# Roots of the norms on GpSimd, late transposes, quartered modulation products and token-by-token ends in a two-layer backbone

## The chip, the cores and the metric

One core of a Trainium2 chip runs the whole program. The metric is device time in microseconds (us), the median of three runs. TensorE (PE, with its weight loads PEld), VectorE (DVE), ScalarE (ACT), GpSimd (POOL) and SyncE (SP, which here only issues DMAs) each work through their own list of instructions in order; semaphores tie the lists together.

## What is computed

Two layers over 640 tokens of width 1024 (128 context tokens, 512 latent tokens). The first layer mixes tokens by attention and by a gated delta rule side by side, the second by a state-space mixer; each is followed by an MLP. Before every mixer and every MLP the tokens are normalised and modulated, and every result is gated into the residual. Cut to what the change touches:

```python
mod = silu(cond) @ w_mod[layer] + b_mod[layer]           # cond: one row for context, one for latent
sh1, sc1, g1, sh2, sc2, g2 = split(mod, 6)
h = rms_norm(x, norm_mix_g[layer]) * (1 + sc1) + sh1     # mean square, root, scale, shift
x = x + g1 * mixer(h)
h = rms_norm(x, norm_mlp_g[layer]) * (1 + sc2) + sh2
x = x + g2 * (square(relu(h @ w_mlp_in)) @ w_mlp_out)
```

After the second layer there is a last norm. The outputs are the tokens, the keys and values of the context, and the final states of both recurrences.

## The kernel before

**Products.** Every 32-bit operand is split into a rounded part and its remainder (`hh`/`hl` for activations, `whi`/`wlo` for weights), and a product is three matmuls. The rounding is a copy on ACT, the remainder a subtraction on DVE (a few on POOL). `stage` makes products that come out with features on partitions (tile `gps`, line 304): blocks of weights are the stationary side, and half of the tokens, 320 or 322 columns, move. The first half covers token tiles 0, 1 and half of 2. Twenty-four matmuls make one block of 128 features for one half.

**by_rows.** The projections back to the residual (`oute` and `outo` behind the mixers, `m2` in the MLP) come out with tokens on partitions (tile `rps`, line 330). The 1024 output columns are made in two halves `hm` of 512. Weights arrive as 1 MB blocks of four rows of 128, split into pairs. For each row and each of the five token tiles there are three matmuls. With `done` given and in the second half, the last eight rows are held, and then each token tile is finished by itself; in all other halves the five tiles grow side by side and finish together. Five of six PSUM banks are filled at a time.

**Norm and modulation.** As a token tile of the second half is finished, `gated` adds it to `x`, `square` sums its squares on ACT, and `done` goes on: after tile 1 (for 0 and 1), after tile 2, and after tile 4 (for 3 and 4) `root` makes the reciprocal roots by three Newton steps (`rsqrt`, lines 238 to 243, all on DVE, nine small operations behind two integer ones), `scaled` multiplies by root and scale (`hrow`, line 402) and adds the shift (line 403), and `turned` transposes eight blocks on PE (tile `hps`, line 409), four at a time, into `hh` (ACT, line 412) and `hl` (DVE, line 413). When tile 4 is done, all the transposes that are left are written into the program before the next stage. This happens at three places: between layer 0's mixer and its MLP (about 604 to 634 us), between the layers (1098 to 1130 us, where `hps` has one PSUM bank), and between layer 1's mixer and its MLP (1736 to 1760 us).

**Modulation vectors.** `mod_first` makes layer 0's first two with `condst`, 32 columns wide, as stationary side; it runs four 128-column quarters of the weights into four groups of 32 PSUM partitions (line 515). The other ones come from `mod_steps`, a generator that is advanced between other work and walks over chunks of 512 columns: two raw blocks of 1 MB each through two landing buffers. For chunks 4 to 9 of layer 0, in the stretch of the delta heads' input products, PE multiplies directly, eight matmuls of 512 columns into 32 partitions a chunk (line 462). For the other fourteen chunks, beside layer 0's MLP, ACT and DVE sum the products with the weights into two accumulators `macc` (four buffers, lines 486 and 489), and PE sums over partitions by two matmuls of 512 columns. `mod_out` adds bias and gain after each chunk and writes 4 KB to DRAM, from which `bands` broadcasts later.

**Layer 1's output projection.** `odd` first loads and splits weights, then makes `yh`/`yl` out of the mixer's result `yt`, and takes the mixer norm's mean squares by fifteen small matmuls (`stc`, line 1413) and its roots `yr` ahead of `by_rows`; `yr` is used in `gated`.

**What sets the order.** The program is written in the order of the code and then put in order for each engine by the framework's scheduler, which goes by its own estimate of times. So a change of one stage can also move instructions of another one.

Of the kernel before, what the change touches and what calls it, by code (L numbers as in the profile page):

```python
# [111 lines left out]
def _rows(i):  # L112

    out, index, pos = [], {}, 0

    def put(key, v):
        nonlocal pos
        index[key] = pos
        out.append(np.asarray(v).reshape(-1))
        pos += out[-1].size  # L120

    for layer in range(2):
        for c in range(12):
            put(("bias", layer, c), np.stack([i["b_mod"][layer, c * 512:c * 512 + 512]] * 2))
        for c in (2, 3, 8, 9):
            gain = i["norm_mix_g" if c < 4 else "norm_mlp_g"][layer]
            put(("gain", layer, c), np.stack([gain[c % 2 * 512:c % 2 * 512 + 512]] * 2))
    put("gfin", i["final_norm_g"])
    return np.concatenate(out), index
# [36 lines left out]
def _consts():  # L166
# [11 lines left out]
    put("ident", np.eye(P))  # L178
    put("stat", np.full((P, 1), 1.0 / 32.0))
# [28 lines left out]
class Prog:  # L208
    def __init__(self, nc, tc, ctx, io, widx, ridx, pidx, cidx, csmall, taps=None):
        self.nc, self.tc, self.ctx, self.io = nc, tc, ctx, io  # L210
        self.turn, self.share = 0, False
        self.behind = None
        self.mlast = None
        self.widx, self.ridx, self.pidx, self.cidx, self.csmall = widx, ridx, pidx, cidx, csmall
        self.taps = taps or {}
# [17 lines left out]
    def rsqrt(self, pool, out, ms, shape, post=1.0):  # L233
# [73 lines left out]
    def stage(self, keys, xs, half, evac, side=None):  # L307

        for i in range(0, len(keys), 2):
# [9 lines left out]
    def by_rows(self, keys, parts, evac, done=None, side=None, pre=()):  # L319
# [12 lines left out]
        for hm in range(2):  # L332
            banks, held = [], []
            for i, key in enumerate(keys(hm)):
# [39 lines left out]
    def norm_rows(self, pool):  # L374
# [8 lines left out]
        def root(a, b):  # L383
            v.scalar_tensor_tensor(out=ms[:, a:b], in0=ss[:, a:b, 0], scalar=EPS, in1=ss[:, a:b, 1], op0=ALU.add, op1=ALU.add)
            self.rsqrt(pool, r[:, a:b], ms[:, a:b], [P, b - a])
# [4 lines left out]
    def modulated(self, pool, scale, shift, h, off, halves):  # L390
# [6 lines left out]
        def scaled(t, r):  # L397
            q = min(t, 1)
            for j in range(2):
                y = halves(t, j)  # L400
                c = slice(j * 512, j * 512 + 512)
                v.scalar_tensor_tensor(out=y, in0=self.x[:, t, c], scalar=r[:, t:t + 1], in1=scale[:, q, c], op0=ALU.mult, op1=ALU.mult)
                v.tensor_tensor(out=y, in0=y, in1=shift[:, q, c], op=ALU.add)
                todo.append((t, 4 * j, y))

        def turned(t, a, y):
            ps = self.pn.tile([P, 512], F32, name="hps", tag="n")
# [7 lines left out]
        def done(t):  # L415
# [15 lines left out]
    def mod_bias(self, layer, c, pool):  # L431

        out = []
        for key in ("bias", "gain")[:2 if (layer, c) in self.gains else 1]:
            x = pool.tile([2, 512], F32, name=f"m{key}", tag=f"m{key}", bufs=2 if key == "bias" else 1)
            o = self.ridx[key, layer, c]
            self.nc.sync.dma_start(out=x, in_=self.io["rows"][o:o + 1024].rearrange("(p x) -> p x", p=2))
            out.append(x)
        return out

    def mod_out(self, layer, c, ps, row, gain=None):

        nc = self.nc
        nc.vector.tensor_tensor(out=row, in0=ps[0:2], in1=row, op=ALU.add)
        if gain is not None:
            nc.vector.scalar_tensor_tensor(out=row, in0=row, scalar=1.0, in1=gain, op0=ALU.add, op1=ALU.mult)
        nc.scalar.dma_start(out=self.modr[layer][c // 2, :, c % 2 * 512:c % 2 * 512 + 512], in_=row)

    def mod_steps(self, todo, landing, small, pool=None, after=None):
# [4 lines left out]
        if pool:  # L454
            sel = pool.tile([P, 2, 32], F32, name="msel")
            nc.vector.memset(sel, 0.0)
            for j in range(2):
                nc.vector.memset(sel[:, j, j:j + 1], 1.0)
        raws, n = [], 2 * len(todo)

        def product(lhs, x, start, stop):
            nc.tensor.matmul(ps, lhs, x, start=start, stop=stop)  # L462

        for i in range(n + 1):
            if i < n:
                layer, c = todo[i // 2]
                raw = landing.tile([P, 2048], F32, name="wraw", tag="wraw")
                o = self.widx["mod", layer, c, i % 2]
                nc.sync.dma_start(out=raw, in_=self.io["wall"][o:o + P * 2048].rearrange("(p x) -> p x", p=P))
                raws.append(raw.rearrange("p (k c) -> p k c", c=512))  # L470
                if i % 2 == 0:
                    nextrows = self.mod_bias(layer, c, small)
            if i:
                layer, c = todo[(i - 1) // 2]
                if i % 2:
                    rows = nextrows
                    ps = self.pmod.tile([P, 512], F32, name="modps", tag="mod")[:32]
                    acc = [pool.tile([P, 512], F32, name="macc", tag="macc", bufs=4) for j in range(2)] if pool else []
                for k in range(0 if i % 2 else 4, 4 if i % 2 else KT):
                    x = raws[i - 1][:, k % 4]  # L480
                    if not pool:
                        product(self.condst[:, k, :], x, k == 0, k == KT - 1)
                    for j, a in enumerate(acc):
                        w = self.condst[:, k, j:j + 1]
# [5 lines left out]
                if i % 2 == 0:  # L490
                    for j, a in enumerate(acc):
                        product(sel[:, j], a, j == 0, j == 1)
                    self.mod_out(layer, c, ps, *rows)
# [1299 lines left out]
```

## Time and profile before

| | us |
|---|---|
| runs of the kernel before | 2224.25, 2229.60, 2221.36 |
| their median | 2224.25 |
| the profiled execution | 2224.19 |
| its span (first to last instruction) | 2222.4 |
| PE busy within the span | 2112.9 |

The profiled execution has 1.8 us outside its span, and stands 0.06 us from the median, so that a sum made on its span can be put on the median as it is. In the rows below, a line such as L304 is a line of the code of before. A matmul of whole 32-bit numbers leaves two records. The clock of a stretch is the share of TensorE's full clock that was granted: 1.00 is 2.4 GHz, and 0.50 is 1.2 GHz.

### The profile page before, as it was taken

What the parts mean: (1) busy time and instruction counts of PE and PEld (TensorE: products, weight loads), DVE (VectorE), ACT (ScalarE), POOL (GpSimd) and SP (SyncE); (2) the same over time, 40 slices, a digit from 0 to 9 for tenths busy, and PEclk for the clock granted to TensorE, in tenths of its full rate; (3) what the DMA queues carried; (4) which work ended last, traced back from release to release, by engine and by line L of the source; (5) the groups of instructions that cost most, each with busy time, mean ns of one, the idle gap of its engine ahead of it and who ended that gap; (6) DMA issues with size and microseconds to landing.
All of it is one profiled execution on the core that took longest, in us unless ns stands there. A gap on an engine that the chain in (4) does not pass through costs nothing.

```text
span 2222.4 us, 32146 instructions
## 1 busy us (share of the span) xinstructions
PE 2112.9 (95%) x12883; PEld 1851.6 (83%) x12883; DVE 1386.5 (62%) x2606; ACT 897.9 (40%) x1892; POOL 151.1 (7%) x112
## 2 busy tenths in 40 slices
PE   6999789998989999999889999999989799999998
PEld 5958687786787888889789999999968698989896
DVE  6355676766589767574667877777642644444445
ACT  4324435345243322313237876667532231313131
POOL 1031220300000000000000101111210000000000
PEclk9999889999999999999989999999989899999999
DMA  7251100004245434332214443333342121212221
GB/s 316 95 190 64 37 1 17 18 1 149 93 152 211 168 133 145 122 133 79 88 46 151 146 145 115 127 119 113 111 173 83 67 95 57 89 63 81 72 76 48
DMA packets 55152, 232.97 MB, mean 105 GB/s; under 512 B 6487, under 2 KB 20799, under 8 KB 33115
## 3 DMA queue, kind: packets, MB, share of 16 engines
q1 hardware_dynamic: 45192, 216.34, 27.6%
q10 hardware_dynamic: 9810, 14.58, 1.9%
q8 instruction: 101, 1.65, 0.3%
q14 instruction: 49, 0.39, 0.1%
HBM read 222.47 MB, written 8.43 MB: 104 GB/s over the span
## 4 chain that ended last, share of the span: by engine, by line
PE 90%; DVE 5%; DMA 2%; ACT 2%; issue 1%; POOL 0%; SPq 0%; DVEq 0%; ACTq 0%; POOLq 0%
PE gps L304 42%; PE rps L330 28%; PE modps L462 3%; PE yps L1695 2%; PE atps L749 2%; PE avps L1326 2%; PE offps L1709 1%; PE stps L1726 1%; DMA X<-growd 1%; PE scps L1268 1%; DMA wraw<-wall 1%; PE dps L1027 1%; PE dps L1033 1%; PE xkps L1545 1%; PE hps L409 1%
## 5 line engine op out<-in xcount | busy, mean ns | idle before, releaser
L304 PE MATMUL gps<-hh,whi 128*128 128x322 f32 (+3 forms) x1552 | 492.4, 318 | 3.3 <-ACT whi L276 2.6
L304 PE MATMUL gps<-hl,whi 128*128 128x322 f32 (+3 forms) x1552 | 487.0, 314 | 0.0
L304 PE MATMUL gps<-hh,wlo 128*128 128x322 f32 (+3 forms) x1552 | 486.0, 314 | 0.0
L304 PEld LDWEIGHTS gps<-hh,whi 128*128 128x128 f32 (+1 forms) x1552 | 293.5, 189 | 18.4 <-issue 7.6
L304 PEld LDWEIGHTS gps<-hl,whi 128*128 128x128 f32 (+1 forms) x1552 | 293.4, 189 | 6.5 <-issue 5.9
L304 PEld LDWEIGHTS gps<-hh,wlo 128*128 128x128 f32 (+1 forms) x1552 | 293.0, 189 | 3.2 <-issue 2.5
L330 PE MATMUL rps<-wlo,hidh 128*128 128x512 f32 x640 | 253.0, 395 | 0.0
L330 PE MATMUL rps<-whi,hidh 128*128 128x512 f32 x640 | 252.3, 396 | 0.0
L330 PE MATMUL rps<-whi,hidl 128*128 128x512 f32 x640 | 251.5, 395 | 0.0
L276 ACT CAST whi<-wraw 128x1024 fp32r<-128x1024 f32 (+2 forms) x132 | 140.0, 1062 | 259.0 <-PE rps L330 178.9
L304 PE MATMUL gps<-yh,whi 128*128 128x320 f32 x1024 | 227.6, 311 | 1.4 <-DVE yh L413 1.4
L288 DVE TENSOR_TENSOR wlo<-wraw,whi 128x1024 fp32r<-128x1024 f32 x88 | 108.9, 1240 | 189.8 <-ACT whi L287 189.7
L279 DVE TENSOR_TENSOR wlo<-wraw,whi 128x1024 fp32r<-128x1024 f32 (+3 forms) x123 | 156.8, 1276 | 106.4 <-ACT whi L276 105.7
L287 ACT CAST whi<-wraw 128x1024 fp32r<-128x1024 f32 x88 | 91.7, 1048 | 276.2 <-PE rps L330 199.3
L304 PEld LDWEIGHTS gps<-yh,whi 128*128 128x128 f32 x1024 | 173.3, 190 | 2.1 <-DVE yh L413 1.8
L304 PE MATMUL gps<-yh,wlo 128*128 128x320 f32 x512 | 159.3, 311 | 0.0
L330 PEld LDWEIGHTS rps<-whi,hidh 128*128 128x128 f32 x640 | 120.2, 188 | 33.4 <-ACT macc L489 4.2
L330 PEld LDWEIGHTS rps<-whi,hidl 128*128 128x128 f32 x640 | 120.2, 188 | 29.0
L330 PEld LDWEIGHTS rps<-wlo,hidh 128*128 128x128 f32 x640 | 120.3, 188 | 28.5
L649 DVE TENSOR_SCALAR hr<-gps 128x320 f32<-128x320 f32 x128 | 62.4, 488 | 119.9 <-PE gps L304 119.9
L486 DVE SCALAR_TENSOR_TENSOR macc<-wraw,condst,macc 128x512 f32<-128x512 f32 x196 | 136.3, 737 | 0.9 <-DMA wraw<-wall 0.7
L650 ACT ACTIVATE hr<-hr 128x320 f32<-128x320 f32 x128 | 59.9, 469 | 166.8 <-DVE hr L649 166.8
(428 smaller groups left out, 3629.7 us busy)
## 6 DMA issues: line engine op xcount, KB each, us to landing
wraw<-wall SPq DMA_DIRECT2D x158, 1024.0 KB
bc<-afs SPq DMA_DIRECT2D x40, 512.0 KB
Q<-afr SPq DMA_DIRECT2D x64, 128.0 KB
xt<-xt ACTq DMA_DIRECT2D x1, 2560.0 KB
X<-growd SPq DMA_DIRECT2D x8, 320.0 KB
x<-x ACTq DMA_DIRECT2D x1, 2560.0 KB
xd<-x ACTq DMA_DIRECT2D x1, 2560.0 KB
x<-xd SPq DMA_DIRECT2D x1, 2560.0 KB
```

Source lines behind the costliest of these rows:

```text
L276: self.nc.scalar.copy(out=hi, in_=raw[:, :, c:c + m])
L279: eng.tensor_tensor(out=lo, in0=raw[:, :, c:c + m], in1=hi.bitcast(F32), op=ALU.subtract)
L287: self.nc.scalar.copy(out=hi, in_=x)
L288: self.nc.vector.tensor_tensor(out=lo, in0=x, in1=hi.bitcast(F32), op=ALU.subtract)
L304: self.nc.tensor.matmul(ps, ws[k // KT][q // 2][:, k % KT, :], xs[q % 2][k][:, c], start=k == 0 and q == 0, stop=k == n - 1 and q == 2)
L330: nc.tensor.matmul(ps, parts[x][k][:, c], w[y][:, j, :], start=k == 0 and q == 0, stop=k == n - 1 and q == 2)
L462: nc.tensor.matmul(ps, lhs, x, start=start, stop=stop)
L486: nc.vector.scalar_tensor_tensor(out=a, in0=x, scalar=w, in1=a, op0=ALU.mult, op1=ALU.add)
L649: nc.vector.tensor_scalar(out=r, in0=ps, scalar1=0.0, scalar2=None, op0=ALU.max)
L650: nc.scalar.activation(out=r, in_=r, func=AF.Square)
L749: nc.tensor.matmul(ps[:, :n], x[k][:, TOFF[t]:TOFF[t] + P], w[:, k, :], start=k == 0 and q == 0, stop=k == KT - 1 and q == 2)
L1326: nc.tensor.matmul(acc, val(c, i), p, start=c == 1, stop=c == 6)
```

## The change

The diff does more than its few words tell. Seven things, by place:

1. The Newton steps of the roots in `modulated` go to GpSimd, where a step takes four operations in place of three (`rsqrt` with `eng`). The last norm and the mixers' own roots stay on DVE.
2. In `by_rows` the last four rows of weights (two pairs) are held in every half, and the token tiles finished one after the other; the last eight stay held where they were.
3. The transposes that are left when tile 4 is done are no longer made there; `late` puts them into the next stage, behind its first products for the first half of the tokens. Between the layers they go through the next stage's three banks.
4. `mod_steps` multiplies by quarters as `mod_first` did, 128 columns into 32 partitions each, and collects all chunks of a layer in one PSUM bank, each chunk in rows of its own.
5. `mod_out` runs once for all chunks of a call, with one tile of biases and gains, and writes four DMAs; the twenty small operations and the small DMAs of the chunks fall away. The accumulators `macc` have one buffer each.
6. The mean squares of layer 1's mixer and `yr` move from ahead of `by_rows` to behind its first half's unheld rows (`mid`).
7. `hrow` gets four buffers of its own beside the weights; the first place's shift comes as four tiles.

```diff
     def rsqrt(self, pool, out, ms, shape, post=1.0, eng=None):
...
         for n in range(3):
+            if eng:
+                eng.tensor_tensor(out=a, in0=out, in1=out, op=ALU.mult)
+                eng.tensor_tensor(out=a, in0=a, in1=ms, op=ALU.mult)
+                eng.tensor_scalar(out=a, in0=a, scalar1=-0.5, scalar2=1.5, op0=ALU.mult, op1=ALU.add)
+                eng.tensor_tensor(out=out, in0=a, in1=out, op=ALU.mult)
+                continue
...
                     evac(2 * i + j, hf, self.gemm(w, xs, hf, half))
+                    if i == hf == 0:
+                        self.late((0, 1, 1, 2)[j])
...
-                    if done and hm and k >= n - KT:
+                    if k >= n - (KT if done and hm else 4):
                         held.append((k, w))
                         continue
...
+            if mid and not hm:
+                mid()
...
-                r = root(a, t + 1)
+                r = root(a, t + 1, nc.gpsimd)
                 for u in range(a, t + 1):
                     scaled(u, r)
-            if t == 4:
-                while todo:
-                    turned(*todo.pop(0))
+            self.turns = todo, turned
...
+    def late(self, n):
+        todo, turned = self.turns
+        for _ in range(min(n, len(todo))):
+            turned(*todo.pop(0))
...
-            nc.tensor.matmul(ps, lhs, x, start=start, stop=stop)
+            for q in range(4):
+                nc.tensor.matmul(ps[32 * q:32 * q + 32], lhs, x[:, q * P:(q + 1) * P], start=start, stop=stop)
...
-                    acc = [pool.tile([P, 512], F32, name="macc", tag="macc", bufs=4) for j in range(2)] if pool else []
+                    acc = [pool.tile([P, 512], F32, name="macc", tag=f"macc{j}") for j in range(2)] if pool else []
...
-                    self.mod_out(layer, c, ps, *rows)
+                    if last:
+                        self.mod_out(layer, cs, ps, band)
...
             first = [(x, self.gemm(x, xs, 0, HP, cols=CCUT[0])) for x in w]
+            self.bank = lambda name: self.ps_x.tile([P, 512], F32, name=name, tag="x")
+            self.late(4)
```

**PE, third place** (before layer 1's MLP): `rps` are the last products of token tile 4, `hps` the transposes, `gps` the MLP's first products. Before:

```order
L330 MATMUL rps<-wlo,yh_15023 128x512
L330 MATMUL rps<-whi,yl 128x512
L409 MATMUL hps<-con,hrow 128x128 x32
L304 MATMUL gps<-yh_15022,whi 128x320
L304 MATMUL gps<-yh_15023,whi 128x320
L304 MATMUL gps<-yh_15022,wlo 128x320
```

And with the change, on PE at the same place:

```order
L334 MATMUL rps<-wlo,yh_15186 128x512
L334 MATMUL rps<-whi,yl 128x512
L415 MATMUL hps<-con,hrow 128x128 x12
L306 MATMUL gps<-yh_15185,whi 128x320 x4
L415 MATMUL hps<-con,hrow 128x128 x4
L306 MATMUL gps<-yh_15186,whi 128x320
L306 MATMUL gps<-yh_15185,wlo 128x320
```

The sixteen transposes of tiles 3 and 4 have left this row of 32; they stand later, four, four and eight together, between the ninety-six matmuls of the first half.

**DVE, third place**, from the root of token tile 2 on (`nr` is the start value of the root, `wlo` are the next stage's weights, `yh_15023` and `yh_15186` are remainders of transposes). Before:

```order
L239 TENSOR_SCALAR nr<-rsi 128x1
L279 TENSOR_TENSOR wlo<-wraw,whi 128x1024
L241 TENSOR_TENSOR rsa<-nr 128x1
L279 TENSOR_TENSOR wlo<-wraw,whi 128x1024
L242 SCALAR_TENSOR_TENSOR rsa<-rsa,nms 128x1
L413 TENSOR_TENSOR yh_15023<-hps,yh_15022 128x4x128 x2
L243 SCALAR_TENSOR_TENSOR nr<-rsa,nr 128x1
L365 SCALAR_TENSOR_TENSOR rps<-rps,yr,gate 128x512
L279 TENSOR_TENSOR wlo<-wraw,whi 128x1024
L241 TENSOR_TENSOR rsa<-nr 128x1
```

And with the change, on DVE:

```order
L235 TENSOR_SCALAR nr<-rsi 128x1
L281 TENSOR_TENSOR wlo<-wraw,whi 128x1024 x3
L419 TENSOR_TENSOR yh_15186<-hps,yh_15185 128x4x128
L371 SCALAR_TENSOR_TENSOR rps<-rps,yr,gate 128x512
L408 SCALAR_TENSOR_TENSOR hrow<-x,nr,band_15243 128x512 x2
L419 TENSOR_TENSOR yh_15186<-hps,yh_15185 128x4x128
```

The small Newton steps, which stood singly between large operations, are gone from DVE, and `hrow` follows five large operations behind `nr`.

**PE, start of the mixers of layer 0** (about 263 us; `dps` and `kvps` belong to the delta heads, `scps` to the attention's scores). Before:

```order
L932 MATMUL dps<-con,dk_957 128x128 x5
L971 MATMUL dps<-dq_961,kT 128x128 x4
L949 MATMUL dps<-kT 128x128 x5
L971 MATMUL dps<-dq_961,kT 128x128
L1258 MATMUL scps<-con,pp 128x128 x2
L1268 MATMUL scps<-kst_1468,qs 128x128
```

And with the change, on PE:

```order
L1279 MATMUL scps<-kst_1587,qm_3150 128x512
L1279 MATMUL scps<-kst_1586,qs 128x256
L1279 MATMUL scps<-kst_1587,qm_3150 128x256
L1279 MATMUL scps<-kst_1586,qs 128x256
L1279 MATMUL scps<-kst_1587,qm_3150 128x256
L943 MATMUL dps<-con,dk_957 128x128 x5
L1279 MATMUL scps<-kst_1586,qs 128x512
```

No line of the delta heads or of the attention was edited, but the scheduler now puts sixteen matmuls of the scores ahead of these five `dps` of the second head, where all of them stood behind.

## Rows read from the trace of the kernel before

**Rows 1.** The page, part 1: busy us, share of the span, instructions.

```profile
PE 2112.9 (95%) x12883; PEld 1851.6 (83%) x12883; DVE 1386.5 (62%) x2606; ACT 897.9 (40%) x1892; POOL 151.1 (7%) x112
```

**Rows 2.** Windows: stretch and length, busy us and instructions by engine, clock, DMA share, GB/s.

```profile
102.00:177.00 75.00, 75.00 (x309) 39.62 (x308) 46.14 (x91) 19.44 (x57) 18.11 (x18) 1.00 0.47 170
177.00:256.00 79.00, 79.00 (x546) 78.88 (x545) 48.86 (x104) 40.05 (x110) 10.17 (x5) 1.00 0.11 41
256.00:303.00 47.00, 27.51 (x136) 25.12 (x135) 35.21 (x73) 16.67 (x51) 26.00 (x21) 0.60 0.16 44
...
604.00:634.00 30.00, 23.07 (x138) 21.79 (x137) 23.71 (x61) 11.93 (x22) 0.00 (x0) 0.83 0.39 141
634.00:1098.00 464.00, 464.00 (x2464) 395.78 (x2463) 323.91 (x507) 142.04 (x231) 0.00 (x0) 1.00 0.38 135
1098.00:1130.00 32.00, 19.88 (x90) 15.34 (x89) 20.42 (x43) 8.88 (x16) 0.00 (x0) 0.70 0.22 86
...
1613.00:1632.00 19.00, 11.82 (x53) 10.02 (x54) 12.40 (x19) 12.71 (x20) 4.64 (x3) 0.73 0.89 331
...
1736.00:1760.00 24.00, 10.51 (x53) 8.36 (x51) 21.98 (x49) 9.85 (x17) 0.00 (x0) 0.71 0.42 154
```

**Rows 3.** Groups by line: busy us, mean ns of one, idle before.

```profile
L462 PE MATMUL modps<-wraw,condst 128*32 128x512 f32 x96 | 43.4, 595 | 0.0
...
L462 PE MATMUL modps<-macc,msel 128*32 128x512 f32 x56 | 27.0, 599 | 0.0
```

**Rows 4.** The chain that ended last: start us, length us, what, records.

```profile
36.82 1.93 PE modps L515 x64
...
102.55 3.55 PE modps L462 x8
...
697.44 1.83 PE modps L462 x4
...
745.34 28.32 PE gps L304 x192
...
1613.45 4.99 DMA wraw<-wall
```

**Rows 5.** Timeline of PE, third place: start us, length us, what, idle before.

```profile
1747.78 1.94 PE L409 MATMUL hps<-con,hrow 128*128 128x128 f32 x8 [7.12 <-DVE hrow L403]
1754.47 1.94 PE L409 MATMUL hps<-con,hrow 128*128 128x128 f32 x8 [4.75 <-DVE hrow L403]
...
1760.32 0.90 PE L304 MATMUL gps<-yh,whi 128*128 128x320 f32 x2 [1.40 <-DVE yh L413]
```

**Rows 6.** Timeline of DVE, third place, root of token tile 2.

```profile
1735.11 0.15 DVE L239 TENSOR_SCALAR nr<-rsi 128x1 int32<-128x1 int32 x1
...
1737.29 1.23 DVE L279 TENSOR_TENSOR wlo<-wraw,whi 128x1024 fp32r<-128x1024 f32 x1
...
1745.54 1.41 DVE L402 SCALAR_TENSOR_TENSOR hrow<-x,nr,band 128x512 f32<-128x512 f32 x2
```

**Rows 7.** Groups by line on POOL.

```profile
L979 POOL TENSOR_TENSOR qd<-qd,dq 128x512 f32<-128x512 f32 x8 | 8.7, 1092 | 7.0 <-DVE dec L978 7.0
...
L942 POOL TENSOR_TENSOR M<-db,con 128x640 f32<-128x640 f32 x4 | 5.1, 1264 | 33.0 <-PE gps L304 18.4 <-PE dps L1141 13.7 <-DVE drs L243 0.9
...
L1241 POOL MEMSET top<- 64x1 f32 x1 | 0.1, 93 | 0.1
```

**Rows 8.** Timeline of DVE and POOL side by side, a delta head's root.

```profile
269.73 0.17 DVE L241 TENSOR_TENSOR rsa<-drs 128x10 f32<-128x10 f32 x1
269.85 1.53 POOL L944 TENSOR_TENSOR M<-M,de 128x640 f32<-128x640 f32 x1 [1.81 <-ACT de L940]
269.94 1.47 DVE L242 SCALAR_TENSOR_TENSOR rsa<-rsa,dss 128x10 f32<-128x10 f32 x1
```

**Rows 9.** Timeline of ACT, start of layer 1's output projection.

```profile
1618.46 1.04 ACT L287 CAST whi<-wraw 128x1024 fp32r<-128x1024 f32 x1 [5.28 <-DMA wraw<-wall]
1619.41 2.60 ACT L1403 CAST yh<-yt 128x640 fp32r<-128x640 f32 x4
```

More of the change, by code (lines that the diff above doesn't have):

```diff
@@ L109, in _stream, with _bands, band @@
     return np.concatenate(out), index
[L112 to L129, printed above, removed]
+def _bands(i):
+    def band(rows):
+        x = np.stack(rows, axis=0).reshape(6, 2, 4, P)
+        o = np.zeros((4, 8, 2, 2, P), np.float32)
+        o[:, :6] = x.transpose(2, 0, 1, 3)[:, :, None]
+        return o.reshape(P, P)
+    one = np.ones(D, np.float32)
+    return np.stack([np.concatenate([
+        band(list(i["b_mod"][layer].reshape(6, D))),
+        band([one, i["norm_mix_g"][layer], one, one, i["norm_mlp_g"][layer], one])], axis=1) for layer in range(2)])
 def _params(i):
@@ L420, in done, with mod_out @@
                 a = 2 if t == 2 else t - 1
-                r = root(a, t + 1)
+                r = root(a, t + 1, nc.gpsimd)
                 for u in range(a, t + 1):
                     scaled(u, r)
-            if t == 4:
-                while todo:
-                    turned(*todo.pop(0))
+            self.turns = todo, turned
         return square, done
[L431 to L447, printed above, removed]
+    def late(self, n):
+        todo, turned = self.turns
+        for _ in range(min(n, len(todo))):
+            turned(*todo.pop(0))
+    def mod_out(self, layer, chunks, ps, band):
+        v = self.nc.vector
+        t = self.small.tile([P, P], F32, name="modt", tag="modt")
+        v.tensor_tensor(out=t, in0=ps, in1=band[:, :P], op=ALU.add)
+        v.scalar_tensor_tensor(out=t, in0=t, scalar=self.cst("scales"), in1=band[:, P:], op0=ALU.add, op1=ALU.mult)
+        r = slice(4 * chunks[0], 4 * chunks[-1] + 4)
+        for q in range(4):
+            self.nc.scalar.dma_start(out=self.modr[layer].rearrange("a b (h q c) -> q (a b h) c", h=2, q=4)[q, r], in_=t[32 * q + r.start:32 * q + r.stop])
     def mod_steps(self, todo, landing, small, pool=None, after=None):
@@ L481, in mod_steps @@
                     if not pool:
-                        product(self.condst[:, k, :], x, k == 0, k == KT - 1)
+                        product(self.condst[:, k, 32 - row:64 - row], x, first and k == 0, last and k == KT - 1)
                     for j, a in enumerate(acc):
-                        w = self.condst[:, k, j:j + 1]
+                        w = self.condst[:, k, 32 + 2 * j:33 + 2 * j]
                         if k:
@@ L491, in mod_steps @@
                     for j, a in enumerate(acc):
-                        product(sel[:, j], a, j == 0, j == 1)
-                    self.mod_out(layer, c, ps, *rows)
+                        r = row + 2 * j
+                        product(sel[:, 32 - r:64 - r], a, first and j == 0, last and j == 1)
+                    if last:
+                        self.mod_out(layer, cs, ps, band)
             yield
@@ L827, in late @@
                 self.padding(np_, h)
-                square, done = self.modulated(np_, scale, shift, h, TOFF, lambda t, j: hid.tile([P, 512], F32, name="hrow", tag="macc", bufs=4))
+                square, done = self.modulated(np_, scale, lambda q, j: shift[:, q, j * 512:j * 512 + 512], h, TOFF)
                 sq.append(square)
@@ L1420, in odd @@
             shift, scale = (self.bands(np_.tile([P, 2, D], F32, name=f"band{kind}"), 1, kind) for kind in (3, 4))
[L1421 to L1422 removed]
+            square, done = self.modulated(np_, scale, lambda q, j: shift[:, q, j * 512:j * 512 + 512], h, [P * t for t in range(NT)])
             def evac(t, hm, ps):
```

98 lines of the change are left out of this document (52 added, 46 removed).

## The prediction

> **What bounds the kernel now.** I read the page's first part first: PE is busy for 2112.9 of 2222.4 us, so 109.5 us are idle on it [rows 1]. Then the windows, to see which stretches those are. From 102 to 256 us, from 634 to 1098 us and in most of the rest PE is busy without a gap at a clock of 1.00 [rows 2]. There only one thing makes the program shorter: less work for PE. The idle time sits at a few places: 19.5 us between 256 and 303, 6.9 at the first place of the norms (604 to 634), 12.1 at the second (1098 to 1130), 7.2 at the start of layer 1's output projection (1613 to 1632) and 13.5 at the third place (1736 to 1760), and in each of them the granted clock is between 0.60 and 0.83, so that part of PE's own work there runs at 1.2 GHz [rows 2]. At those places only what PE waits for counts. So the change has to be read twice: as PE work removed from full stretches, and as waits moved at the five places.
>
> **Term 1, direct modulation products (102 to 177 us).** Before, a raw block costs PE eight records in 3.55 us, and there are twelve of them (96 records): 42.6 us [rows 3, 4]. After, a raw block is sixteen matmuls of 128 columns into 32 partitions. That form is in the trace already: 64 records, which are 32 matmuls, take 1.93 us [rows 4]; sixteen take 0.97, twelve blocks 11.6. That is 31.0 us less on an engine that has no gap there. The cover that may be gone is the DMA's. A raw block on its own takes 4.99 us from issue to landing [rows 4], there are two landing buffers, and a new load goes out when PE has finished the block two before. By the order, PE has between that moment and the product 6 to 10 us of work (the products of one block and 30 to 70 matmuls at 28.32 / 192 = 0.148 us each [rows 4], and some transposes). So a lone load fits, but three weight blocks share the stretch, and the traffic of 170 GB/s there [rows 2] has to come in 45 us instead of 75, near 290 GB/s. DVE's 46.1 us [rows 2] also get squeezed. If all thirteen loads behind the first two came one at a time, they would need 13 x 5.0 = 65 us where PE has 45: 20 us lost. Lower bound none. I take 6 us, nearer to none since the lone load fits. Term 1: -25 us (-31 to -11).
>
> **Term 2, products of the accumulators (634 to 1098 us).** Fourteen chunks at 1.83 us (four records; 56 in all) become eight quarter matmuls, 8 / 32 x 1.93 = 0.48 us [rows 3, 4]. 14 x 1.35 = 18.9 us, with PE busy for 464 of 464 us [rows 2]. The single accumulator buffer makes ACT's first product of a chunk wait for PE's sum of the one before; in the order these sums stand 21 to 42 us of PE work apart, while a chunk needs 14 operations on DVE. I take this wait as covered; if the cover is gone, about 1 us for each chunk on ACT and then PE. Term 2: -19 us (-19 to -6).
>
> **Term 3, token by token in every half.** PE does the same matmuls, and at the ends of halves in that stretch PE has no gap today [rows 2]. So finishing tiles earlier brings nothing. It keeps two pairs of weights for up to 60 matmuls longer; with five buffers the next half's first pair sits in the fifth, and the others come free some 60 matmuls before their use. The one tight case is the second half of `oute`, whose last pair needs a buffer that is free only at the end of the half before, 18 matmuls ahead of its use. 0 (0 to +5).
>
> **Term 4, third place.** Today the transposes of tile 2 start at 1747.78, those of tiles 3 and 4 at 1754.47, and the MLP's first product at 1760.32 [rows 5]. With the change the products follow the transposes of tile 2, and 3 and 4 have 96 matmuls (14 us) to become ready in. The transposes of tile 2 wait for `hrow`, which starts 10.4 us behind `nr` (1735.11 to 1745.54) because the Newton steps stand between large DVE operations [rows 6]. After, five such operations stand between them, three of them `wlo` of 1.23 us [rows 6]: near 5 us. In that time GpSimd must make twelve small operations. The trace has none of two inputs and one column. Bounds: a memset of one column takes 0.093 us, a two-input operation of 512 columns 1.09, of 640 columns 1.26 [rows 7]. The last two lie on a line of 1.3 ns for each column, which leaves 0.4 us at no column; that is my value, an estimate: 12 x 0.4 = 4.9 us, just about the 5. I put `hrow` 2.5 us earlier, as more of tile 2's and 1's work stands behind it in line on DVE. The first products can then start some 3.3 us behind those transposes, at 1748.5 instead of 1760.3; 2 us for the sixteen transposes now among them go off, and 2 for DVE's queue. Term 4: -8 us (-12 to -3).
>
> The Trainium skill speaks against this part: GPSIMD Engine Reference, section 4.1, sends elementwise work on a tile to VectorE, since GpSimd takes about twice as long with two inputs. By it a step's operation would cost twice VectorE's 0.17 us, the root 4.1 us instead of my 4.9, and the sum would stay within 1 us for each place.
>
> **Term 5, the other places.** Second place: of 12.1 idle us [rows 2] the last part is the four rounds of transposes for tiles 3 and 4 through one bank; they now go through three banks behind the first products. The start, up to tile 2, keeps its one bank. -7 us (-10 to -2), with the second drop of the clock. First place: here the products already run between the transposes, and by the order DVE now does sums of `macc` ahead of the last remainder that the second half of tokens needs. 0 (-4 to +6). Start of the output projection: `yh` stood on ACT behind a `whi` that waited 5.28 us for its load [rows 9]; in the new order all `yh` stand ahead of that `whi`. Then DVE's remainders are last, near 1617 instead of 1620. -2.5 us (-6 to 0). The end of the program (last norm on DVE) keeps its order.
>
> **Term 6, the mixers of layer 0.** Nothing is edited, but the order moves. PE now has sixteen score matmuls ahead of the delta work that it waited for between 256 and 303, where 19.5 us are idle at a clock of 0.60 [rows 2]. What is brought forward is missing later as filler, and the chains of the heads stay as long as they are. I take 8 of the 19.5. No row excludes a loss: bounds -25 (all of the gap and the clock) and +12 (as much again lost behind as I gain in front, and some). Term 6: -8 us.
>
> **Sum.** 25 + 18.9 + 0 + 8 + 7 + 0 + 2.5 + 8 = 69.4. On the profiled execution's 2224.2 us, which stands at the median, that makes 2154.8, so 2155 us.
>
> **Rivals.** (a) *PE is no longer what the first stretch waits for.* The quarters free 31 us, but loads, or the remainders on DVE, hold the stretch at its length. For it: two landing buffers, 290 GB/s wanted. Against it: 4.99 us for a load where PE's work lasts 6 to 10. All 31 gone gives 2155 + 25 = 2180. (b) *The new order of layer 0's mixers loses.* For it: the scheduler goes by its own estimate, and gaps that are filled early open later. Against it: the gap at 256 to 303 is the largest one of the program. At +12 the time is 2155 + 20 = 2175; the other end, -25, gives 2138. (c) *The roots on GpSimd become the bound, and the kernel gets slower.* The mechanism: while GpSimd works on two inputs, a DVE operation of that kind stands still. A DVE step of 0.17 us took 1.47 us beside one of GpSimd's [rows 8], and the reverse holds, so that the twelve operations and the large DVE ones take turns. Nine roots lie at the three places. At 1.09 us an operation, the price of 512 columns [rows 7], a root costs 13.1 us in place of about 2; nine of them exposed are +100 us, so 2255. It passes today's time when a root costs 2 + 69.4 / 9 = 9.7 us, or 0.8 us an operation, and all nine are exposed. Against it: tiles 3 and 4 now have 14 us of products as cover, and the first root stands ahead of tile 2's twenty-four matmuls; with the second root alone exposed at that price it is 2155 + 33 = 2188, still faster. The same page of the Trainium skill, section 1 (Specifications), lists SBUF interfaces that GpSimd shares with VectorE, with contention for VectorE instructions of two SBUF inputs; the rows on the 1.47 us agree. (d) *The change does not do what its words say.* Finishing token by token removes no wait where PE is full [rows 2]; this I hold to be so, and it is in the sum as 0.
>
> **Chances and range.** Forecast, 2140 to 2170: 0.58. Better than that, down to 2117 (term 6 at its good end): 0.08. Rival (a): 0.14. Rival (b), alone or with part of (a), up to 2195: 0.14. Near today's time, by several terms at their poor ends: 0.04. Rival (c) in full: 0.02. The range from 2130 to 2188 leaves out the lowest part of the good end, the highest of (a) with (b), and the last two, together under 0.2. Half a per cent, 11 us, is about what can be told from no change here; all but the last two cases lie beyond it: faster 0.94, same 0.04, slower 0.02.
>
> **What would show it.** Right: the stretch up to 256 us ends near 231; modulation products take some 12 and 7 us of PE; the MLP of layer 0 is shorter by 19 us without gaps; at the third place PE's products start within 2 us behind the transposes of tile 2, and those of 3 and 4 stand between them. Wrong: PE waits for `wraw` or `wlo` between 102 and 150 us (rival a); more waits of PE between the start of the mixers and layer 0's output projection than before (rival b); operations on GpSimd of over 0.8 us in the roots, with DVE operations stretched beside them (rival c). A stage that gets slower by a cause that is none of these, say the transposes' banks taken from the state-space mixer, would make the sum wrong as a whole.

## The result and the profile after

The changed kernel takes 2154.2 us (median of four runs, 2149.6 to 2155.5) where the kernel before took 2226.9 us beside it: a ratio of 0.967, 95% interval 0.963 to 0.970. The forecast was 2155.0 us. Its profiled span is 2152.4 us against 2222.4, so 70.0 us are to be explained. One later run of the changed kernel took 3376.8 us, at a granted clock of 0.55 where its other runs have 0.97 to 0.98; it goes into no comparison. The engine line of its page, the answer to [rows 1]:

```profile
PE 2059.8 (96%) x13339; PEld 1851.4 (86%) x13339; DVE 1365.1 (63%) x2504; ACT 896.6 (42%) x1892; POOL 178.7 (8%) x220
```

PE is busy for 53.1 us less; the other 16.9 us are idle time of PE. To see where, I cut both traces at the same PE instructions: the first direct modulation product, the first score of the mixers, the first `rps` of layer 0's output projection, the first `hps`, the first `rps` of the MLP, the first `hps` of the second place, the first and the last product of the state-space mixer (between them nothing changes, 413.9 and 414.2 us), the first `hps` and the first MLP `rps` of the third place (the MLP behind it takes 392.9 us in both). Windows of the kernel before (length, busy us and count for each engine, PEclk, DMA share, GB/s):

```profile
102.48:255.59 153.11, 153.11 (x846) 117.80 (x846) 94.37 (x192) 58.81 (x166) 27.87 (x23) 1.00 0.29 104
255.59:550.12 294.53, 257.82 (x1718) 213.27 (x1716) 203.38 (x543) 130.75 (x344) 53.08 (x41) 0.90 0.12 38
550.12:605.35 55.23, 55.23 (x229) 44.60 (x230) 30.79 (x52) 15.74 (x27) 0.00 (x0) 0.96 0.28 96
605.35:683.28 77.93, 71.00 (x445) 65.91 (x443) 68.77 (x132) 32.55 (x58) 0.00 (x0) 0.93 0.46 164
683.28:1097.94 414.66, 414.66 (x2151) 350.56 (x2150) 278.18 (x433) 120.07 (x193) 0.00 (x0) 1.00 0.37 130
1097.94:1197.53 99.59, 87.47 (x544) 81.21 (x542) 62.78 (x120) 43.89 (x100) 3.62 (x3) 0.90 0.29 96
...
1611.47:1736.42 124.95, 116.87 (x506) 95.53 (x503) 55.11 (x91) 33.66 (x51) 6.23 (x4) 0.95 0.31 114
1736.42:1819.44 83.02, 69.20 (x435) 67.19 (x434) 44.53 (x86) 30.25 (x54) 0.00 (x0) 0.88 0.24 84
```

The same windows of the changed kernel:

```profile
101.12:225.17 124.05, 122.74 (x1134) 118.05 (x1134) 91.03 (x186) 58.74 (x166) 33.36 (x28) 1.00 0.36 129
225.17:515.52 290.35, 261.42 (x1712) 217.88 (x1710) 199.19 (x528) 131.29 (x344) 47.29 (x36) 0.90 0.11 35
515.52:571.80 56.28, 56.27 (x238) 45.41 (x239) 33.53 (x57) 16.36 (x28) 3.58 (x13) 0.97 0.34 114
571.80:649.59 77.79, 69.16 (x465) 66.67 (x463) 65.09 (x111) 31.90 (x58) 5.30 (x24) 0.93 0.49 179
649.59:1049.55 399.96, 399.96 (x2299) 352.01 (x2298) 265.56 (x407) 118.52 (x193) 3.29 (x17) 1.00 0.37 133
1049.55:1144.04 94.49, 83.72 (x542) 78.46 (x540) 62.14 (x108) 46.65 (x105) 6.99 (x22) 0.93 0.28 101
...
1558.20:1677.14 118.94, 114.88 (x511) 94.27 (x507) 54.32 (x82) 36.67 (x54) 10.81 (x18) 0.99 0.33 120
1677.14:1749.32 72.18, 66.76 (x431) 64.87 (x430) 41.58 (x67) 28.57 (x53) 6.19 (x23) 0.93 0.27 96
```

Read row by row: the stretch of the modulation products is 29.1 us shorter, the mixers 4.2, layer 0's output projection and the first place together 0.9 longer, the MLP 14.7 shorter, the second place 5.1, layer 1's output projection 6.0, the third place 10.8. Length less PE's busy time is what PE waits: in the mixers 36.7 us before and 28.9 after, at the third place 13.8 and 5.4.

### The profile page after: what moved, and what is told of

Same layout as the page of the kernel before. It is cut to its first block, busy times and chain, and to the rows that moved or that the text cites. A ratio compares the mean times of both kernels' runs of the same rounds, so it can differ in the third digit from the quotient of the medians.

```text
span 2152.4 us, 32997 instructions
## 1 busy us (share of the span) xinstructions
PE 2059.8 (96%) x13339; PEld 1851.4 (86%) x13339; DVE 1365.1 (63%) x2504; ACT 896.6 (42%) x1892; POOL 178.7 (8%) x220
## 4 chain that ended last, share of the span: by engine, by line
PE 87%; DVE 7%; DMA 3%; ACT 1%; issue 1%; POOL 1%; ACTq 0%; SPq 0%; DVEq 0%; POOLq 0%
PE gps L306 41%; PE rps L334 27%; PE atps L756 2%; PE yps L1710 2%; PE avps L1337 2%; DMA wraw<-wall 1%; PE offps L1724 1%; PE scps L1279 1%; DMA X<-growd 1%; PE dps L1044 1%; PE stps L1741 1%; PE dps L1038 1%; PE xkps L1560 1%; PE modps L465 1%; DMA bc<-afs 1%
## 5 line engine op out<-in xcount | busy, mean ns | idle before, releaser
L334 PEld LDWEIGHTS rps<-whi,hidh 128*128 128x128 f32 x640 | 120.3, 188 | 29.3 <-issue 1.2
L334 PEld LDWEIGHTS rps<-whi,hidl 128*128 128x128 f32 x640 | 120.3, 188 | 28.8
```

Of the source, the lines that this page charges most:

```text
L334: nc.tensor.matmul(ps, parts[x][k][:, c], w[y][:, j, :], start=k == 0 and q == 0, stop=k == n - 1 and q == 2)
```

## Experiments

Each is an edit of the changed kernel, but `quarters`, which is one of the kernel before. Ratios are to the kernel before, run beside it on the same chip. The changed kernel itself came twice more: as `again`, at 0.965 (0.962 to 0.968), where the profiled run was the one of 3376.8 us, so that its stages can't be read, and as `after2`, at 0.964 (0.961 to 0.967); the second profile of it is that of `after2`, with a span of 2152.2 us.

> The changed kernel, nothing edited, for a second undisturbed profile of it. In the three experiments that have the same order of layer 0's mixers on PE that stage took 287.4 us, in the first profile of this kernel 290.4, with equal idle time of PE (28.7 to 28.9 us) and 42 against 48 us of work at the half clock. Theory: where the clock falls within a stage differs from execution to execution, so the mixers come out between 287 and 291 here with 28.8 us idle, and no edit explains those 3 us. Rival: the Newton steps on GpSimd or the finishing by tiles cost the mixers 3 us; then they take 290.4 again.

The mixers took 290.38 us again, with 29.08 us idle. That alone would have spoken for the rival, but `turn_end`, `two_banks`, `root_double` and `first_end` settle it: all have GpSimd's steps and the finishing by tiles, and took 290.6, 290.4, 284.7 and 284.9 us. So the rival is wrong: the stage's length differs from execution to execution.

**The products alone (`quarters`).**

```diff
-    nc.tensor.matmul(ps, lhs, x, start=start, stop=stop)
+    for q in range(4):
+        nc.tensor.matmul(ps[32 * q:32 * q + 32], lhs, x[:, q * P:(q + 1) * P], start=start, stop=stop)
...
-        self.mod_out(layer, c, ps, *rows)
+        if last:
+            self.mod_out(layer, cs, ps, band)
```

> The kernel before with parts 4 and 5 of the change alone: the modulation products in quarters and one bank, their result taken out once for each layer; the four buffers of the accumulators, the norms, the halves and the transposes are those of before. Theory: these two parts bring all of the first stretch (153.1 to 124.1 us), 14 x 1.26 = 17.6 us by the accumulators and the 4.2 us of the mixers, whose order on PE is the same here as in the changed kernel; the rest belongs to the places of the norms. Span 2222.4 - 29.1 - 17.6 - 4.2 = 2171 (2168 to 2175). Rival: the parts only work together (what the products free is lost again at the places as long as those are unchanged): span above 2178, or the mixers back at 294 us.

Measured: 2171.8 us, 0.973 (0.970 to 0.976), span 2164.8. Its windows of the modulation products, the mixers, the first place, the MLP and the third place:

```profile
101.49:225.53 124.04, 122.82 (x1134) 118.05 (x1134) 91.05 (x186) 58.72 (x166) 33.39 (x28) 1.00 0.37 129
225.53:513.01 287.48, 258.69 (x1713) 216.24 (x1711) 199.24 (x529) 131.32 (x344) 47.43 (x36) 0.91 0.11 36
...
568.37:643.31 74.94, 68.02 (x469) 65.49 (x467) 66.11 (x129) 32.41 (x58) 0.00 (x0) 0.95 0.46 168
643.31:1042.05 398.74, 398.74 (x2296) 351.26 (x2295) 270.49 (x422) 119.13 (x193) 0.00 (x0) 1.00 0.38 137
...
1679.61:1761.86 82.25, 68.43 (x435) 66.42 (x434) 44.54 (x86) 30.30 (x54) 0.00 (x0) 0.88 0.24 85
```

The theory holds in kind: two of the seven parts bring 57.6 of the 70.0 us by the profiles, and by the ratios 2.7 of 3.5 per cent (`again`, on the same chip). The mixers follow from them (28.8 us idle, as with the whole change), and the third place stays as it was. The span came 3 us under my range, by the mixers (287.5, not 290.4); but the profiled run is the fastest of four, and the other three took 2170.5 to 2173.2 us, which is within the range.

**Newton steps back on VectorE (`root_dve`).**

```diff
-    r = root(a, t + 1, nc.gpsimd)
+    r = root(a, t + 1)
```

> The changed kernel with part 1 undone: the Newton steps of the nine roots on VectorE again. Theory A (the prediction's reason): the steps stand in VectorE's line between large operations and keep hrow back there, so this costs 1 to 3 us at the first and at the third place and about nothing at the second: span 2155 to 2160. Theory B: VectorE waits for GpSimd anyway (1.30 us idle ahead of hrow at the first place, 0.97 at the second, 0.73 and 1.16 at the third), and a root on GpSimd takes 3.3 to 6.1 us, so that it costs nothing or less on VectorE: span 2147 to 2152, the places together no longer than now.

Measured: 2150.3 us, 0.964 (0.961 to 0.967), beside 0.965 for the changed kernel: no difference that can be told. The mechanism of theory A is nevertheless there. Third place, VectorE, from the root's start value to `hrow`, in `root_dve`:

```profile
1671.53 0.15 DVE L235 TENSOR_SCALAR nr<-rsi 128x1 int32<-128x1 int32 x1
...
1682.10 1.41 DVE L408 SCALAR_TENSOR_TENSOR hrow<-x,nr,band 128x512 f32<-128x512 f32 x2
```

In the changed kernel, on GpSimd and VectorE:

```profile
1675.41 0.15 DVE L235 TENSOR_SCALAR nr<-rsi 128x1 int32<-128x1 int32 x1
1675.70 1.23 DVE L281 TENSOR_TENSOR wlo<-wraw,whi 128x1024 fp32r<-128x1024 f32 x1
1675.70 1.27 POOL L238 TENSOR_TENSOR rsa<-nr 128x1 f32<-128x1 f32 x1 [7.47 <-DVE nr L235]
1677.05 0.19 POOL L239 TENSOR_TENSOR rsa<-rsa,nms 128x1 f32<-128x1 f32 x1
...
1681.86 1.42 DVE L408 SCALAR_TENSOR_TENSOR hrow<-x,nr,band 128x512 f32<-128x512 f32 x2 [0.73 <-POOL nr L241]
```

`hrow` starts 10.6 us behind the start value on VectorE, as before [rows 6], and 6.5 us with GpSimd. PE's idle time at the place falls from 7.4 to 5.4 us by it. But the place is as long (72.5 and 72.2 us): one wait of PE has become several, and more of its work falls at the half clock. At the first place GpSimd costs: 131.5 us with the output projection in `root_dve`, 134.1 in the changed kernel.

**Held weights as before (`held_old`).**

```diff
-    if k >= n - (KT if done and hm else 4):
+    if done and hm and k >= n - KT:
```

> The changed kernel with part 2 undone: only the last half ahead of a norm is finished tile by tile, every other half weight by weight. Theory (the prediction's): no wait of PE hangs on it; layer 0's output projection gets back the 1.0 us that it lost (56.3 to 55.2), layer 1's stays at 118.9, the MLPs at 400.0 and 392.9; span 2150 to 2153. Rival: finishing by tiles is what made layer 1's output projection shorter by 6.0 us; then it goes back to 122 to 125, and the span is 2155 to 2159.

Measured: 2152.6 us, 0.965 (0.961 to 0.968). Layer 0's output projection stayed at 56.3, so the 1.0 us there was not this part's (it is 55.4 in `root_dve`); layer 1's took 120.3, the MLPs 400.8 and 392.9. The finishing by tiles brings nothing that can be told from zero.

**Longer roots (`root_double`).**

```diff
-    for n in range(3):
+    for n in range(6 if eng else 3):
```

> The changed kernel with six Newton steps on GpSimd in each of the nine roots instead of three (the last three change nothing in the value): a root takes 12 x 0.275 = 3.3 us longer. Theory: of the three roots of a place only the second (tile 2) is exposed, since the first lies beside the products of the last half and the third beside 14 us of the next stage's products: 3 x 3.3 = 10 us and the clock that follows idle time, span 2160 to 2167. Rival (c) of the prediction takes all nine as exposed: 9 x 3.3 = 30 us, span 2180. A third case: none is exposed, since other work fills the place: 2150 to 2155.

Measured: 2159.1 us, 0.968 (0.965 to 0.971). What PE waited for at the three places, first in the changed kernel, then in `root_double` (engine, line, waited for: us, times, longest):

```profile
PE hps L415 <- DVE hl L419: 7.2, 2, 4.8
...
PE hps L415 <- DVE hl L419: 7.8, 4, 3.0
...
PE hps L415 <- DVE yh L419: 3.8, 2, 2.8
```

```profile
PE hps L415 <- DVE hl L419: 11.5, 3, 6.3
...
PE hps L415 <- DVE hl L419: 10.5, 5, 4.7
...
PE hps L415 <- DVE yh L419: 8.7, 2, 7.7
```

By the windows PE's idle time grew by 3.6, 3.3 and 3.4 us at the three places, 10.3 us in all, which is the theory's number. (The mixers were 5.6 us shorter here by the clock; without that the span is 2162.4.) But the mechanism was not the theory's. The roots of tiles 0 and 1 took 6.6 us in place of 3.2, as expected. Those of tile 2 took 12.0, 10.2 and 13.4 us where they had taken 5.1, 3.2 and 6.1: in the new order they start within 0.1 us of the end of the root before, beside VectorE's `hrow` and `wlo`, and 22 of their 72 operations took 0.51 to 2.97 us instead of 0.19. The longest one, at the third place, on GpSimd and VectorE:

```profile
1677.97 1.88 DVE L409 TENSOR_TENSOR hrow<-hrow,band 128x512 f32<-128x512 f32 x3
1678.08 2.97 POOL L241 TENSOR_TENSOR nr<-rsa,nr 128x1 f32<-128x1 f32 x1
1679.78 1.22 DVE L281 TENSOR_TENSOR wlo<-wraw,whi 128x1024 fp32r<-128x1024 f32 x1
```

The nine roots together became 42 us longer, and 10.3 us of that show as idle time of PE. So they are exposed in part only, which rules out that all nine are exposed in full; that it is one root of three is not shown. The whole became 7.2 us longer than `after2`, beside it on the same chip. The waits name `hl` and not `hrow`, since the subtraction that frees a PSUM bank stands behind `hrow` in VectorE's line, and `hrow` waits for GpSimd.

**Transposes at the end again (`turn_end`), and at the first place alone (`first_end`).**

```diff
                 for u in range(a, t + 1):
                     scaled(u, r)
+            if t == NT - 1:
+                while todo:
+                    turned(*todo.pop(0))
             self.turns = todo, turned
```

> The changed kernel with part 3 undone: the transposes of tiles 3 and 4 are written at the end of the place again, ahead of the next stage's products. Theory A (the prediction's): the third place lives on this part (term 4), so it goes back from 72.2 towards 83.0 us, and the second place from 94.5 to 99.6: span 2164 to 2168. Theory B: in the built order only the second place differs on PE, and the products stand ahead of those transposes at the third place anyway; then the second place alone loses about 5 us, the third keeps its 72 us, and the span is 2155 to 2159.

Measured: 2163.3 us, 0.969 (0.965 to 0.972), span 2161.4. The third place takes 83.5 us again, so theory A holds there, and theory B is wrong: the transposes of tiles 3 and 4 stand ahead of the products again. PE at the third place in `turn_end` (start, us, what; idle before it and who ended it):

```profile
1685.90 1.12 PE L415 MATMUL hps<-con,hrow 128*128 128x128 f32 x4 [1.23 <-DVE yh L419]
1693.62 1.94 PE L415 MATMUL hps<-con,hrow 128*128 128x128 f32 x8 [6.61 <-DVE hrow L409]
1696.11 1.97 PE L415 MATMUL hps<-con,hrow 128*128 128x128 f32 x8 [0.55 <-DVE yh L419]
1699.48 0.90 PE L306 MATMUL gps<-yh,whi 128*128 128x320 f32 x2 [1.40 <-DVE yh L419]
```

In the changed kernel the products stand where this one waits 6.6 us for the `hrow` of tiles 3 and 4:

```profile
1685.82 1.09 PE L415 MATMUL hps<-con,hrow 128*128 128x128 f32 x4 [0.71 <-DVE hrow L409]
1687.58 1.43 PE L306 MATMUL gps<-yh,whi 128*128 128x320 f32 x4 [0.68 <-ACT yh L418]
1688.81 1.05 PE L415 MATMUL hps<-con,hrow 128*128 128x128 f32 x4
```

The second place lost 1.7 us without the late transposes, and the first place gained: 129.0 us with the output projection instead of 134.1. So I tried that alone, with the added lines for the first place only.

> The changed kernel with part 3 undone at the first place alone: there the transposes of tiles 3 and 4 stand at the end of the place again; at the second and the third place they stay among the next stage's products. With part 3 undone everywhere the output projection and the first place of layer 0 together took 129.0 us where the changed kernel takes 134.1, and the third place 83.5 where it takes 72.2. Theory: both effects are local, so that here the first place has its 129.0 and the third keeps its 72.2 us: span 2147 (2144 to 2149). Rival: the 5 us at the first place are the clock's (9.5 us of work at the half clock against 6.3) and come and go with where it falls, so the two stages are back at 132 to 134 us and the span is 2150 to 2154.

Measured: 2147.8 us (2143.5 to 2150.7), 0.965 (0.963 to 0.968), span 2141.6; the two stages take 129.2 us, the third place 71.9. Both effects are local, and by the stages the theory holds. The ratio does not tell the whole from the changed kernel (0.964 to 0.967): the profiled run is the second fastest of five, and 5.4 of its 10.8 us against the first profile are the mixers'. What late transposes cost at the first place is seen in the changed kernel on VectorE and PE: the subtraction that frees the bank stands behind sums of the accumulators, and PE waits 2.5 us among the first products.

```profile
599.99 1.40 DVE L491 SCALAR_TENSOR_TENSOR macc<-wraw,condst,macc 128x512 f32<-128x512 f32 x2
601.31 0.48 DVE L643 TENSOR_TENSOR hidl<-hr,hidh 128x320 fp32r<-128x320 f32 x1
601.71 0.68 DVE L419 TENSOR_TENSOR hl<-hps,hh 128x512 fp32r<-128x512 f32 x1
```

```profile
602.45 0.66 PE L415 MATMUL hps<-con,hrow 128*128 128x128 f32 x4 [2.47 <-DVE hl L419]
```

**A second bank at the second place (`two_banks`, `mixed`, `mixed_plain`).**

```diff
+    def bank(name):
+        n[0] += 1
+        return self.pmod.tile([P, 512], F32, name="modps", tag="mod") if n[0] % 2 else self.pn.tile([P, 512], F32, name=name, tag="n")
+    self.bank = bank
```

> The changed kernel, with the transposes of the second place taking turns between their one bank and the bank of the modulation products, which are over by then. PE waits there 7.8 us in four waits for hl, the subtraction on VectorE that frees the one bank. Theory: the bank is what it waits for; the waits shrink to 2 to 4 us, the second place from 94.5 to 89 to 91 us, span 2146 to 2149. Rival: VectorE is behind in any case (six subtractions of 0.69 us and twelve operations for hrow stand in its line); then PE waits as long, now for hrow, and the span stays at 2150 to 2154.

Measured: 2151.5 us, 0.964 (0.961 to 0.967), the rival's time. The 7.8 us of waits for `hl` became 2.7 us (0.5 for the old bank, 2.2 for the second), as the theory has it, but 3.3 us of waits for `hrow` came in their place, as the rival has it. The place takes 93.6 us, which the time of the whole does not show.

> The changed kernel with part 3 undone at the first place alone, and with the transposes of the second place taking turns between two banks. Alone, the second bank made the second place 0.9 us shorter, with 1.9 us less idle time on PE. Theory: the two add up: span 2146 (2143 to 2148). Rival: the second bank only moves the wait from hl to hrow and the clock takes the rest, so that this is no faster than with the first place's transposes alone: 2147 to 2150.

`mixed` is `first_end` with the second bank. Measured: 2145.4 us (2141.4 to 2146.1), 0.964 (0.962 to 0.966). All four runs lie below all eleven runs of the changed kernel that went into the comparisons (2148.1 to 2155.5); the ratios, taken on different chips, don't tell the two apart. The first place kept its 73.0 us, the second fell to 90.2, more than the bank alone gave. Why, I did not settle; in `mixed_plain` below, with the same two edits in it, that place takes 93.0 us, so it may not be a gain of the two together.

> The kernel with the first place's transposes at its end and two banks at the second, and in it parts 1 and 2 of the change undone together: the Newton steps on VectorE, tile by tile only in the last half ahead of a norm. Each of the two alone, undone in the changed kernel, left the time where it was. Theory: they bring nothing together either; the first place loses about 1 us without GpSimd (quarters, that has both undone, took 130.3 us there with the output projection, first_end 129.2), the third has 2 us more idle time: span 2141 to 2149, median 2143 to 2149. Rival: each covers for the other (the tiles that come early feed roots that come early), so that without both the places are 3 us longer each: span above 2151.

Measured: 2145.4 us (2142.7 to 2148.2), 0.961 (0.959 to 0.964), span 2141.7. The theory holds: with two of the four edits in the title undone, the time is the same.

**The mixer norm's root ahead again (`stc_first`):** the call of `mid` and what it does, moved back ahead of `by_rows`.

> The changed kernel with part 6 undone: the mean of squares and the root of layer 1's mixer norm stand ahead of the output projection again, not between its halves. In the built order ACT still has two whi ahead of the first yh, as in the changed kernel, and not five as before. Theory: PE's wait at the start of that projection (4.06 us, before 7.39) hangs on that order alone, so it stays at 4.1 us and the stage at 119 to 121: span 2150 to 2155. Rival: the fifteen small matmuls and the squares in front of the projection are what made PE wait longer before; then the wait is 7.2 us again and the span 2155 to 2159.

Measured: 2153.2 us, 0.968 (0.966 to 0.971); PE's wait at the start of the projection is 4.06 us. The theory holds. The wait goes with the order on ACT, not with the small matmuls. The first lines there in the changed kernel, where [rows 9] showed a `whi` that waited 5.28 us for its load ahead of `yh`:

```profile
1560.18 1.99 ACT L289 CAST whi<-wraw 128x1024 fp32r<-128x1024 f32 x2 [4.04 <-DVE yt L1545]
1562.08 2.60 ACT L1417 CAST yh<-yt 128x640 fp32r<-128x640 f32 x4
```

That order is there with part 1, 2, 3 or 6 undone, one at a time, and it isn't there in `quarters`. That points at part 7, which was not tried alone, so the cause of the order stays open.

## Why the prediction was right

| term | predicted | measured | by |
|---|---|---|---|
| 1, direct products | -25 | -29.1 | 153.1 to 124.1 |
| 2, accumulators' products | -18.9 | -17.6 | 14 x (1.83 - 0.57) |
| 3, token by token | 0 | 0 | `held_old` |
| 4, third place | -8 | -10.8 | 83.0 to 72.2 |
| 5, second place | -7 | -5.1 | 99.6 to 94.5 |
| 5, first place | 0 | +3.4 | 133.2 to 134.1, with 2.5 of term 2 in it |
| 5, start of the projection | -2.5 | -6.0 | 125.0 to 118.9 |
| 6, mixers | -8 | -4.2 | 294.5 to 290.4 |
| the rest | 0 | -0.6 | start -1.4, others |
| sum | -69.4 | -70.0 | |

That the total came within 1 us is luck: the terms that came out better make 11 us more than forecast, the others 10 us less, and the mixers alone differ by 6 us between profiles of the same order. What was right is the mechanism of the large terms, 1, 2 and 4.

**Term 1.** The products cost what their rows said: PE is busy 30.4 us less, and the stretch ends at 225 us, not at 231. The 6 us of stalls that I took were too many; PE waits 1.3 us in the whole stretch, once, for `vt` on VectorE. Rival (a) is wrong. The first 45 us of the stretch, in the changed kernel:

```profile
101.12:146.12 45.00, 43.69 (x544) 39.86 (x544) 41.17 (x83) 19.41 (x58) 17.33 (x18) 1.00 0.74 268
```

The traffic came at 268 GB/s, near the 290 that I held against it, and PE waited for no load.

**Term 2.** A chunk of quarters takes PE 0.57 us in the chain of waits (`modps` x16), not 0.48, so it saves 1.26 us. The step that failed is the scaling 8 / 32 of a run of 32. Two of the fourteen lie at the first place, twelve in the MLP's window, where PE is busy throughout as forecast; the single buffer of the accumulators cost PE nothing.

**Term 3** held, by `held_old` and by the last MLP's 392.9 us in both.

**Term 4.** The products start at 1687.6, 1.8 us behind the start of tile 2's transposes, within the 2 us asked for. The larger half of the forecast was the products ahead of tiles 3 and 4, and `turn_end` shows it to be all: 11.3 us come back without it. `hrow` did come 4 us earlier by GpSimd, but `root_dve` shows that this moves the place by 0.3 us.

**The root's price.** Of 108 operations on GpSimd all but five take about 0.19 us (0.275 us from start to start), so an undisturbed root takes 3.3 us, not my 4.9: the 0.4 us that I took from the line of 1.3 ns a column is twice too high. The five took 1.04 to 1.28 us, each beside a `wlo` on VectorE (above, 1.27 us beside one of 1.23), and the roots of tile 2 at the first and third place became 5.1 and 6.1 us long. The Trainium skill's factor of two (GPSIMD Engine Reference, section 4.1) shows at neither price: VectorE's own step takes 0.15 to 0.16 us at this size (`root_dve`). The Trainium skill's remark on the shared SBUF interfaces (the same page, section 1) fits the five; here it was GpSimd that waited, and `wlo` kept its 1.23 us.

**Rival (c)** did not come, but I had only half of the reason. Its mechanism is there in part (five operations above 0.8 us; none of VectorE's was stretched), and little of it is exposed: in `root_double` 42 us of longer roots made 10.3 us of idle time. At that share, an estimate from this one run, the nine roots would have to take some 31 us longer each to eat up 70 us.

**Term 5.** The first place lost 3.4 us where I had none, within its range, for the cause I named (sums of `macc` ahead of the last remainder), and GpSimd's root adds to it. The start of the projection gained by the cause I named, but more: 4.0 us of idle time, and 2 us by less work at the half clock in this profile. What shortened the second place is not settled: 1.7 us of it are the late transposes'.

**Term 6.** PE's idle time in the mixers fell by 7.8 us, which is the 8 that I took. But PE's work at the half clock, summed from the trace's clock record, grew from 37 to 48 us in this profile, and 3.6 us of the gain were given back. I had priced the idle time without the clock, and the clock differs from execution to execution: in the twelve profiles of the new order the stage is 3.9 to 10.0 us shorter than in the one profile of before, so one profile's 4.2 us neither bear out the 8 nor refute it. Rival (b) is wrong: none of the twelve is longer than before.

## What to carry to other kernels

First read what work an engine that is always busy no longer has to do, and only then what a place waits for: 46.7 us of the 70 came from matmuls of 512 columns into 32 partitions, of which a chunk's four records took 1.83 us and sixteen records of quarters 0.57. At a place that waits, give PE the next products ahead of the work that isn't ready; but look at every place by itself, since the same edit gained 11 us at the third and lost 5 at the first. Shortening a chain by moving its small operations to an idle engine is worth only what the last wait of the place shows, and here that was nothing.

## What was not expected of the hardware

The same order of the mixers took between 284.6 and 290.7 us in twelve profiles, in three groups near 284.7, 287.4 and 290.5, with PE idle for 27.2 to 30.8 us: what differs most is how much of PE's work falls at 1.2 GHz (31 to 48 us). So two profiles of a stage with many short waits can differ by 6 us without any edit.

A one-column operation on GpSimd beside a `wlo` on VectorE took about as long as that one, 1.27 us for 0.19, while VectorE was not slowed. But this was not so beside every operation of VectorE. Third place of the changed kernel:

```profile
1678.63 1.23 DVE L281 TENSOR_TENSOR wlo<-wraw,whi 128x1024 fp32r<-128x1024 f32 x1 [0.32 <-ACT whi L278]
1678.72 1.20 POOL L238 TENSOR_TENSOR rsa<-nr 128x1 f32<-128x1 f32 x1
1679.78 0.68 DVE L419 TENSOR_TENSOR yh<-hps,yh 128x512 fp32r<-128x512 f32 x1
1679.99 0.19 POOL L239 TENSOR_TENSOR rsa<-rsa,nms 128x1 f32<-128x1 f32 x1
```

Both of VectorE's operations have two inputs, but `wlo` has both in SBUF, and `yh` has one in PSUM. All five slow operations lie beside a `wlo`; 21 that ran beside an operation with an input in PSUM (`hl`, `yh`, `rps`) kept their 0.19 us. The length of VectorE's operation is not what tells them apart: in `root_double` operations were held up for 0.51 us and more beside `hrow`, which is 0.68 to 0.78 us long and has both inputs in SBUF. And the wait can outlast one operation: there one took 2.97 us, through three `hrow` and a `wlo` in a row.
